# Buffers, root operations, weight-part order and store queues in a two-layer encoder kernel

## The chip, the cores and the metric

The kernel runs on one core of a Trainium2 chip. The metric is the device time of one launch in microseconds (us). The profile calls the engines PE (TensorE: matrix products; PEld is its weight load), DVE (VectorE), ACT (ScalarE), POOL (GpSimd) and SP (SyncE, which here only issues DMAs). SPq and ACTq are the parts of SP and ScalarE that issue DMAs.

## The reference

One inference step of a two-layer encoder on 1024 prompt frames and 64 frames of a running stream, 1088 columns in all, 1024 features each, in float32. Layer 0 is a state-space mixer, layer 1 is banded attention; each is followed by a gated feed-forward block (FFN). Norms stand ahead of and behind every block. Cut to what the change touches:

```python
def rmsnorm(x, w):
    y = x * lax.rsqrt(jnp.mean(x * x, axis=-1, keepdims=True) + EPS)
    return y * w

def swiglu(u, w_in, w_out):                 # w_in: 1024 x 5632, w_out: 2816 x 1024
    g, up = jnp.split(u @ w_in, 2, axis=-1)
    return (jax.nn.silu(g) * up) @ w_out

def shared_kv(x, kv_norm_w, w_kv):
    kv = (rmsnorm(x, kv_norm_w) @ w_kv).reshape(b, L, 2, ATT_HEADS, ATT_HEAD_DIM)
    return kv[:, :, 0], kv[:, :, 1]

# one layer, mix = ssd_mixer (layer 0) or the band attention of q, k, v (layer 1):
x = x + rmsnorm(mix(rmsnorm(x, nw[0])), nw[1])
x = x + rmsnorm(swiglu(rmsnorm(x, nw[2]), w_in, w_out), nw[3])
```

The K, Q and V of layer 1 are made from the stream after layer 0, 16 heads of 64.

## The kernel before, in words

Every tensor lies with features on the partitions and the 1088 columns along the free side. A float32 product runs as three passes on TensorE: each operand is split into a high part (a cast to fp32r, on ScalarE) and a low part (what is left, a subtraction on VectorE), and hi·hi, hi·lo and lo·hi are summed in PSUM. In `W.part` (L386, L387) this is done for weights: `hl` or `half` is the split, `raw` the loaded weight, `tt` a sum of weight blocks.

The order of TensorE's instructions is written out by the program: a stream of products, and small tasks (`st.spawn`, `st.run`) that are put between them at planned times. The other engines' order is set by a scheduler which builds each queue from the same program by data readiness and priority (`tc.high_priority(n)`; HIP is 3000). An engine then works through its queue strictly in order and waits at the head of it.

**FFN.** The columns go in two parts, b=0 and b=1 (`HO`, 544 columns in two halves each). The hidden features are 22 tiles. Products are built in 2x2 blocks with seven block products instead of eight (P1 to P7), for which sums of weight blocks and of activation blocks are formed ahead. `T_PLAIN` are the six tiles which run without that scheme for b=0 at the start (`plain_pairs`); `T_BOTH` are the 16 tiles that run in the scheme for both parts, "first pair" being the first of them; `T_TAIL` are the six plain tiles' b=1 parts, which run at the end of the up-projection, the tail. `W` makes the weight blocks' sums and splits, at priority `W.pri`; their keys are names of blocks ("ta", "tb" are sums). `op_build` makes the activation blocks: `total` forms sums and `split` the two parts (cast L1247, subtraction L1248), with priority `OPP`. In `run_pair` the gates and their products are evicted (L1427 to L1444: `p`, `c`, `u`, `x`). `hidden` takes the finished hidden tile, forms four sums of its blocks on GpSimd (L1481), and stores seven blocks to DRAM (L1475, `hscr`), on ScalarE's DMA queue for `T_PLAIN` tiles and on SP's for the others. For the down-projection they are loaded again (L1512) and split (L1518, L1519), partly while the tail still runs. SP's queue also loads the weights (L283), each of which waits for a free `raw` buffer.

**Attention entry.** In `back`, four column quarters q=0..3 of layer 0's result are finished. `rb_steps` calls `rstd` for the inverse root of the mean square: a reduction and L576 on VectorE, then seven small VectorE operations (L580 to L588: a bit-trick start and a cubic polynomial) on a tile of 2 or 3 columns, `nv`, into `nr`; `bcast` spreads `nr` over the partitions through TensorE (`nbp`, L594) and a ScalarE copy. Then the projections follow in three column slices of up to 384. Their evictions `evk`, `evq` and `evv` multiply the PSUM tile by the root into `kf`, `qf` and `vt` (L1898, L1924, L1952), which share one ring of tiles, tag "kqv". `kf` and `qf` are split further into K, Qh and Ql (copies among partitions on SP, L1930), `vt` is transposed, and `kf` and `vt` are also stored as outputs (L492). `cr` and `Cv` are loads of the cached keys and values, `Ck` the cast keys (L1869); `bias` tiles are loaded and partly set by GpSimd memsets (L1885, L1886). The attention task computes scores (L1990), exponentials (L2004) and transposes (`ptp`, L2020).

Of the kernel before, what the change touches and what calls it, by code (L numbers as in the profile page):

```python
# [16 lines left out]
P = 128  # L17
D = 1024
# [22 lines left out]
NS = mybir.DependencyInfo(mybir.DependencyClass.NoSync, mybir.DependencyReason.DATA)  # L41
# [9 lines left out]
EP_W, ER_W, EQ_W = (6.0, 5.0, 8.0, 6.0), (6.0, 4.0, 6.0, 5.0), (16.0, 11.5, 18.0, 16.0)  # L51
# [201 lines left out]
class Weights:  # L253
# [4 lines left out]
    def __init__(self, nc, raw, hl, half, tt):  # L258
        self.nc, self.raw, self.hl, self.half, self.tt = nc, raw, hl, half, tt

        self.tc, self.pri, self.nsc = None, 0, 0
        self.lq, self.sq, self.ready, self.eng = [], [], [], None

        self.raws, self.lent = [raw], None

        self.hx, self.used = Ring(None, "hx", 0, hl.shape, hl.dtype), []

# [99 lines left out]
    def part(self, it, key, ring, v, eng=None, acc=None):  # L367
        if it.get("held"):
            ring = self.held
        elif ring is not self.half:  # L370
            ring = self.hl if ring or self.hl.free() else self.hx
            self.used.append(ring)
        t, n = ring.get(), v.shape[1]
        h, lo = t[:, 0, :n], t[:, 1, :n]
        if it.get("acc"):
            acc = it["src"][0]
        if acc is not None and acc is not False:

            with self.tc.high_priority(self.pri):
                self.nc.scalar.copy(h, v)  # L380
                self.nc.scalar.activation(lo, h, AF.Copy, scale=-1.0)
            self.nc.gpsimd.dma_start(lo, acc, accum_op=ALU.add)
            it[key] = h, lo
            return
        with self.tc.high_priority(self.pri):
            self.nc.scalar.copy(h, v)  # L386
            (eng or self.eng or self.nc.vector).tensor_tensor(lo, v, h, op=ALU.subtract)  # L387
        it[key] = h, lo

# [33 lines left out]
def hybrid_kernel(  # L423
# [60 lines left out]
    def paced(x):  # L484
        if at_pe[0] is not None:
            tc.add_manual_dep(x.ins, at_pe[0].ins.name, NS, reason="pace")
        return x
# [68 lines left out]
            A.activation(q[:, :n], src, AF.Square)  # L556
            (eng or G).tensor_tensor(ssum[:, :n], ssum[:, :n], q[:, :n], op=ALU.add)  # L557

    def rstd(ssum, inv, r, nb, more=None):

        sp = ax("nst")
        if more is None:
            for i in range(nb):
                PE.transpose(sp[:, i * P:(i + 1) * P], ssum[:, i * P:(i + 1) * P], ident)
        else:
            for j, t in enumerate((ssum, more)):
                for i in range(nb):
                    c = 4 * j + i
                    PE.matmul(sp[:, c:c + 1], t[:, i * P:(i + 1) * P], ones[:, 0:1], start=True, stop=True)
        with tc.high_priority(HIP):  # L570
            v = nss.tile([P, 12], F32, tag="nv", bufs=2, name="nv")
            a, h, y = v[:, 0:nb], v[:, 4:4 + nb], v[:, 8:8 + nb]
            if more is None:
                sums = sp[:, :nb * P].rearrange("p (a b) -> p a b", b=P)
                V.tensor_reduce(a, sums, axis=mybir.AxisListType.X, op=ALU.add)
                V.tensor_scalar(a, a, inv, EPS, op0=ALU.mult, op1=ALU.add)  # L576
            else:
                V.tensor_scalar(a, sp[:, :nb], inv, EPS, op0=ALU.mult, op1=ALU.add)
                V.scalar_tensor_tensor(a, sp[:, 4:4 + nb], inv, a, op0=ALU.mult, op1=ALU.add)
            V.tensor_scalar(y.bitcast(I32), a.bitcast(I32), -0.5, float(0x5F3759DF), op0=ALU.mult, op1=ALU.add)  # L580
# [7 lines left out]
            V.scalar_tensor_tensor(r, a, RP[3], y, op0=ALU.add, op1=ALU.mult)  # L588
# [8 lines left out]
        A.activation(rb[:, :n], bp[:, a:a + n], AF.Copy, scale=RL)  # L597
        return rb[:, :n]

    def rb_steps(ssum, n, out, wait=None, rb=None, more=None):  # L600

        nb = (n + P - 1) // P
        nr = nss.tile([P, 4], F32, tag="nr", bufs=2, name="nr")
        rstd(ssum, 1.0 / D, nr[:, :nb], nb, more)
# [610 lines left out]
    def op_build(ops, done, when=lambda: True):  # L1215
# [22 lines left out]
        def split(nm_, keep=False):  # L1238
            if nm_ == "a21":
                yield 0, 0, lambda: R.free(2)  # L1240
                got = [(R.get(), R) for _ in range(2)]
            else:
                yield 0, 0, lambda: some(2)
                got = [take(*rings) for _ in range(2)]
            h, l_ = (rr(v4(t, n)) for t, _ in got)
            with tc.high_priority(OPP[ops.layer][ops.b]):
                A.copy(h, L[nm_])  # L1247
                V.tensor_tensor(l_, L[nm_], h, op=ALU.subtract)  # L1248
# [206 lines left out]
    def back(layer, start, cpost, xsrc, xmid, cpre, cpost2, xout, rb_out, done2):  # L1455
# [3 lines left out]
        with ExitStack() as es:  # L1459
# [6 lines left out]
            def hidden(t_, b, x, z, late=None):  # L1466
# [5 lines left out]
                    st.spawn(store(i, t), HST)  # L1472

                def store(i, t):
                    paced((A if t_ in T_PLAIN else nc.sync).dma_start(hc[:, i, k, HO[b]:HO[b] + n], t))  # L1475
                    stored[i, b] = stored.get((i, b), 0) + 1
                    return
                    yield
# [64 lines left out]
            def end(q, y, ss, more=None):  # L1543
# [76 lines left out]
                    if q in qs and all(x in parts for x in qs):  # L1620
                        done2.append(s)
                yield (0, EQ_W[q]) if q < 3 else (0, 0, lambda: "k2" in done2)
                yield from rb_steps(tot, n, [], ER_W[q], rb_out[:, o:o + n])
                roots.append(q)
                for s, qs in enumerate(((0, 1), (1, 2), (2, 3))):
                    if q in qs and all(x in roots for x in qs):
# [2 lines left out]
            with e2:  # L1629
# [25 lines left out]
                for t_, bs, ends in [(t_, (0, 1), (0,) if t_ == T_BOTH[-1] else ()) for t_ in T_BOTH] + [(t_, (1,), (1,) if t_ == T_TAIL[-1] else ()) for t_ in T_TAIL]:  # L1655
# [4 lines left out]
                        t_, W.get(), bs, ends, ops, lambda *a: hidden(*a, late=late[1] if one else None), px, tmp,  # L1660
                        t_ == T_BOTH[0], late[0] if one else None,
                    )
                    W.pri = 0
                    if t_ == T_BOTH[-1]:
                        phase[0] = 1
                        W.lent.cap = 2
# [181 lines left out]
    with ExitStack() as es:  # L1848
# [41 lines left out]
        def evk(j):  # L1890
            d = kqv[j]

            def f(s, p_):
                n = SL[s][1]
                st.wait_for(lambda: ("rb", s) in done)
                kf = sb2.tile([P, 384], F32, tag="kqv", bufs=2, name="kf")
                with tc.high_priority(HIP):
                    V.tensor_tensor(kf[:, :n], p_[:, :n], rba[s][:, :n], op=ALU.mult)  # L1898
                if not d["Kt"]:
# [13 lines left out]
        def evq(j):  # L1913
            def f(s, p_):
# [4 lines left out]
                if s == 2:  # L1919
                    for q_ in Q[0] + Q[1]:  # L1920
                        G.memset(q_[:, n:].bitcast(F32), 0.0)
                qf = sb2.tile([P, 384], F32, tag="kqv", bufs=2, name="qf")
                with tc.high_priority(HIP):
                    V.scalar_tensor_tensor(qf[:, :n], p_[:, :n], 0.125, rba[s][:, :n], op0=ALU.mult, op1=ALU.mult)  # L1924
                for e in range(2):
# [20 lines left out]
        def evv(j):  # L1946
            def f(s, p_):
                o, n = SL[s]
                st.wait_for(lambda: ("rb", s) in done)
                vt = sb2.tile([P, 384], F32, tag="kqv", bufs=2, name="vt")  # L1950
                with tc.high_priority(HIP):
                    V.tensor_tensor(vt[:, :n], p_[:, :n], rba[s][:, :n], op=ALU.mult)  # L1952
                if s == 1:
# [391 lines left out]
```

## Time and profile before

| | |
|---|---|
| median of 3 runs | 2901.99 us (2899.79 to 2910.09) |
| the profiled execution | 2901.95 us, span 2900.2 us, mean granted clock 0.996 |
| TensorE busy | 98% of the span, 22096 matmuls |
| VectorE busy | 77%, 4767 instructions |
| ScalarE busy | 46%, 2411 |
| GpSimd busy | 26%, 927 |
| DMA | 443.22 MB, 153 GB/s in the mean |

A busy time is summed over an engine's instructions. A wait row names the waiting instruction, the one that released it, and the total, number and longest of such waits. In the timeline a row is start, duration, engine, line, operation, output and inputs; in brackets stands the idle time ahead of it and its releaser. The granted clock is the share of full speed that TensorE got. On the profile's clock layer 0's first pair lies at 905 to 935 us and its tail at 1255 to 1330; the attention entry at 1540 to 1625; layer 1's first pair at 2235 to 2265 and its tail at 2585 to 2660.

### The profile page before, as it was taken

How to read it: one execution, taken by the hardware profiler on the slowest of the kernel's cores; microseconds unless marked ns; L12 is line 12 of the kernel's file. 1: busy time of each engine (PE TensorE's matmuls, PEld its weight loads, DVE VectorE, ACT ScalarE, POOL GpSimd, SP SyncE). 2: the span in 40 equal slices, each digit the busy share in tenths (PEclk: the TensorE clock that was granted, in tenths of full speed). 3: DMA queues.
4: the chain of work that ended last, by engine and by line, in shares of the span. 5: the costliest groups of instructions: out<-in, count | busy, mean ns of one | idle time of the engine just before them, and what ended most of it. 6: DMA issues, size and time to landing. Idle time of an engine off the chain costs nothing. (4 is left out here: it accounts for less than half of the span.)

```text
span 2900.2 us, 57727 instructions
## 1 busy us (share of the span) xinstructions
PE 2843.5 (98%) x22096; PEld 2799.6 (97%) x22096; DVE 2242.8 (77%) x4767; ACT 1347.7 (46%) x2411; POOL 763.6 (26%) x927
## 2 busy tenths in 40 slices
PE   8999999999999999999999999999999999999999
PEld 8999999999999999999999899999999999999998
DVE  7987888786768877787678777777778877787456
ACT  6654646454444222235444455555664322234342
POOL 1343333330123434342022000000032434343012
PEclk9999999999999999999999999999999999999999
DMA  4433333235565455557875432223367454565555
GB/s 134 129 103 99 106 102 108 89 121 159 171 175 165 156 172 168 175 192 262 288 226 179 131 91 77 66 66 89 98 213 217 148 177 148 183 201 191 193 184 159
DMA packets 284789, 443.22 MB, mean 153 GB/s; under 512 B 25696, under 2 KB 231488, under 8 KB 283104
## 3 DMA queue, kind: packets, MB, share of 16 engines
q1 hardware_dynamic: 269184, 417.27, 44.8%
q0 software_dynamic: 3232, 10.56, 2.0%
q10 hardware_dynamic: 12096, 11.70, 1.2%
q8 instruction: 173, 2.83, 0.4%
q14 instruction: 104, 0.85, 0.1%
HBM read 321.34 MB, written 113.63 MB: 150 GB/s over the span
## 5 line engine op out<-in xcount | busy, mean ns | idle before, releaser
L531 PE MATMUL mm<-r,hl 128*128 128x384 f32 (+2 forms) x1672 | 556.4, 333 | 6.1 <-DVE kf L1898 5.0
L533 PE MATMUL mm<-r,hl 128*128 128x384 f32 (+2 forms) x1672 | 539.2, 322 | 1.2 <-DVE hl L387 0.7
L532 PE MATMUL mm<-r,hl 128*128 128x384 f32 (+2 forms) x1672 | 539.0, 322 | 0.0
L1416 PE MATMUL px<-r,hl 128*128 128x288 f32 (+1 forms) x1184 | 348.1, 294 | 0.0
L531 PEld LDWEIGHTS mm<-r,hl 128*128 128x128 f32 x1672 | 316.4, 189 | 8.7 <-DVE kf L1898 5.7
L1417 PE MATMUL px<-r,hl 128*128 128x288 f32 x1056 | 312.4, 296 | 5.4 <-DVE hl L387 5.4
L533 PEld LDWEIGHTS mm<-r,hl 128*128 128x128 f32 x1672 | 315.6, 189 | 1.9 <-DVE hl L387 1.0
L532 PEld LDWEIGHTS mm<-r,hl 128*128 128x128 f32 x1672 | 316.6, 189 | 0.3
L1415 PE MATMUL px<-r,hl 128*128 128x288 f32 x1056 | 311.7, 295 | 2.1 <-DVE u L1430 1.6
L387 DVE TENSOR_TENSOR hl<-raw,hl 128x1024 fp32r<-128x1024 f32 (+2 forms) x186 | 209.5, 1128 | 118.4 <-ACT hl L386 118.1
L557 POOL TENSOR_TENSOR ssum<-ssum,sq 128x256 f32<-128x256 f32 (+1 forms) x111 | 124.5, 1122 | 562.6 <-ACT sq L556 547.8
L386 ACT CAST hl<-raw 128x1024 fp32r<-128x1024 f32 (+2 forms) x186 | 177.4, 954 | 125.2 <-PE po L1758 66.9
L1416 PEld LDWEIGHTS px<-r,hl 128*128 128x128 f32 x1184 | 223.1, 188 | 0.0
L1417 PE MATMUL px<-rx,hl 128*128 128x256 f32 x768 | 214.8, 280 | 6.5 <-DVE hl L387 6.5
L1415 PE MATMUL px<-rx,hl 128*128 128x256 f32 x768 | 214.4, 279 | 1.3 <-DVE x L1389 1.3
L1417 PEld LDWEIGHTS px<-r,hl 128*128 128x128 f32 x1056 | 199.4, 189 | 6.4 <-DVE hl L387 6.4
L1415 PEld LDWEIGHTS px<-r,hl 128*128 128x128 f32 x1056 | 199.5, 189 | 3.3 <-DVE u L1430 2.1
L1756 PE MATMUL po<-r,hl 128*128 128x288 f32 (+1 forms) x682 | 196.8, 288 | 0.0
L1757 PE MATMUL po<-r,hl 128*128 128x288 f32 (+1 forms) x682 | 196.4, 288 | 0.0
L1758 PE MATMUL po<-r,hl 128*128 128x288 f32 (+1 forms) x682 | 196.4, 288 | 0.0
L1416 PE MATMUL px<-rx,hl 128*128 128x256 f32 x640 | 178.9, 280 | 0.0
L2004 ACT ACTIVATE sc<-sc,mx 128x640 f32<-128x640 f32 (+3 forms) x144 | 101.8, 707 | 107.9 <-DVE mx L1999 102.2
(444 smaller groups left out, 8436.6 us busy)
## 6 DMA issues: line engine op xcount, KB each, us to landing
raw<-in_w_f_dram SPq DMA_DIRECT2D x104, 512.0 KB, 4.0
wsum<-in_w_f_dram SPq DMA_DIRECT2D x128, 176.0 KB, 3.7
wscr<-wsum SPq DMA_DIRECT2D x128, 176.0 KB, 3.3
raw<-in_w_in_dram SPq DMA_DIRECT2D x40, 512.0 KB, 3.7
MT<-ascr SPq DMA_DIRECT2D x48, 384.0 KB, 4.2
raw<-in_w_so_dram SPq DMA_DIRECT2D x32, 512.0 KB, 3.9
r<-hscr SPq DMA_DIRECT2D x22, 576.0 KB, 6.2
hl<-kscr SPq DMA_DIRECT2D x11, 1024.0 KB, 5.2
```

Source lines behind the costliest of these rows:

```text
L386: self.nc.scalar.copy(h, v)
L387: (eng or self.eng or self.nc.vector).tensor_tensor(lo, v, h, op=ALU.subtract)
L531: PE.matmul(ps[:, :n], h_, xh, start=(first and i == 0), stop=False)
L532: PE.matmul(ps[:, :n], h_, xl, start=False, stop=False)
L533: at_pe[0] = PE.matmul(ps[:, :n], l_, xh, start=False, stop=(last and i == nk - 1))
L557: (eng or G).tensor_tensor(ssum[:, :n], ssum[:, :n], q[:, :n], op=ALU.add)
L1415: PE.matmul(ps, wh, ah[:, k, :], start=(k == 0), stop=False)
L1416: PE.matmul(ps, wh, al[:, k, :], start=False, stop=False)
L1417: at_pe[0] = PE.matmul(ps, wl, ah[:, k, :], start=False, stop=(k == 3))
L1756: PE.matmul(ps[:, :n], wh, xh, start=(k == 0), stop=False)
L1757: PE.matmul(ps[:, :n], wh, xl, start=False, stop=False)
L1758: at_pe[0] = PE.matmul(ps[:, :n], wl, xh, start=False, stop=(k == KH - 1))
```

## The change

It has five parts. The "kqv" ring has four buffers instead of two. The roots at the attention entry (`rb_out`) are computed on GpSimd: the seven VectorE operations become eleven, since each scalar_tensor_tensor becomes two operations. A split of b=1's activation blocks in `op_build` is ordered behind the last "tb" cast (an order in ScalarE's queue, no wait between engines). `W.pri` is 1000 and no longer 0 from the second pair on. The stores of `hidden` for b=1 go by SP's queue also for `T_PLAIN` tiles.

```diff
         with self.tc.high_priority(self.pri):
-            self.nc.scalar.copy(h, v)
+            last = self.nc.scalar.copy(h, v)
+            if key == "tb":
+                self.last = last
             (eng or self.eng or self.nc.vector).tensor_tensor(lo, v, h, op=ALU.subtract)
...
+            if eng is not None:
+                eng.tensor_scalar(y.bitcast(I32), a.bitcast(I32), -0.5, float(0x5F3759DF), op0=ALU.mult, op1=ALU.add)
+                eng.tensor_tensor(h, y, y, op=ALU.mult)
+                eng.tensor_tensor(h, h, a, op=ALU.mult)
+                for i, p in enumerate(RP):
+                    eng.tensor_scalar(a, a if i else h, p, None, op0=ALU.add)
+                    eng.tensor_tensor(r if i == 3 else a, a, y if i == 3 else h, op=ALU.mult)
+                return
             V.tensor_scalar(y.bitcast(I32), a.bitcast(I32), -0.5, float(0x5F3759DF), op0=ALU.mult, op1=ALU.add)
...
             with tc.high_priority(OPP[ops.layer][ops.b]):
-                A.copy(h, L[nm_])
+                first = A.copy(h, L[nm_])
+                if ops.b and W.last is not None:
+                    tc.add_manual_dep(first.ins, W.last.ins.name, NS, reason="order")
                 V.tensor_tensor(l_, L[nm_], h, op=ALU.subtract)
...
-                    paced((A if t_ in T_PLAIN else nc.sync).dma_start(hc[:, i, k, HO[b]:HO[b] + n], t))
+                    paced((A if t_ in T_PLAIN and not b else nc.sync).dma_start(hc[:, i, k, HO[b]:HO[b] + n], t))
...
-                yield from rb_steps(tot, n, [], ER_W[q], rb_out[:, o:o + n])
+                yield from rb_steps(tot, n, [], ER_W[q], rb_out[:, o:o + n], eng=G)
...
-                    W.pri = 0
+                    W.pri = 1000
...
-                kf = sb2.tile([P, 384], F32, tag="kqv", bufs=2, name="kf")
+                kf = sb2.tile([P, 384], F32, tag="kqv", bufs=4, name="kf")
...
-                qf = sb2.tile([P, 384], F32, tag="kqv", bufs=2, name="qf")
+                qf = sb2.tile([P, 384], F32, tag="kqv", bufs=4, name="qf")
...
-                vt = sb2.tile([P, 384], F32, tag="kqv", bufs=2, name="vt")
+                vt = sb2.tile([P, 384], F32, tag="kqv", bufs=4, name="vt")
```

The order of TensorE's instructions is the same in both kernels. VectorE has 28 instructions fewer, ScalarE's queue 42 DMAs fewer, SP's 42 more, GpSimd 44 operations more. The changed kernel's lines are two to twelve higher (L386 stays, L1247 becomes L1257, L1475 becomes L1487, L1518 L1530, L492 L494, L1884 L1896).

ScalarE's queue at layer 0's first pair, before. The casts of L1247 are b=1's; `tt_11088` is the last "tb" sum.

```order
L386 CAST hl_11168<-tt_11087 128x1024
L380 CAST half_11243<-raw_11102 128x512
L1247 CAST r_11256<-r_9050 128x1152
L381 ACTIVATE half_11243<-half_11243 128x512
L1475 DMA hscr0_114<-x_10942 128x256
L1475 DMA hscr0_114<-sg_11080 128x256
L1247 CAST r_11283<-r_9051 128x1152
L1247 CAST r_11314<-r_11065 128x1152
L386 CAST hl_11236<-tt_11088 128x1024
```

The same place after:

```order
L386 CAST hl_11168<-tt_11087 128x1024
L380 CAST half_11243<-raw_11102 128x512
L1487 DMA hscr0_114<-x_10942 128x256
L381 ACTIVATE half_11243<-half_11243 128x512
L1487 DMA hscr0_114<-sg_11080 128x256
L386 CAST hl_11236<-tt_11088 128x1024
L1257 CAST r_11256<-r_9050 128x1152
L1439 COPY p1_11266<-px_11249 128x256
L1257 CAST r_11283<-r_9051 128x1152
```

The cast of `tt_11088` now stands ahead of three of the L1247 casts, which were ahead of it.

ScalarE's queue in the tail of layer 0, before. `p`, `px` are evictions of the pair, `hl`, `half` weight parts, `hscr` the stores.

```order
L1475 DMA hscr_114<-c_15756 128x288
L1475 DMA hscr_114<-rx 128x288
L1433 ACTIVATE p_15816<-p_15816 128x288
L386 CAST hl<-rx 128x1024
L386 CAST hl<-tt 128x1024 x2
L1443 ACTIVATE px<-px 128x288
L386 CAST half<-raw 128x512
L1427 COPY p_15947<-px 128x288
L1475 DMA hscr_114<-c_15887 128x288
L1475 DMA hscr_114<-rx 128x288
```

The same place after:

```order
L1439 COPY p_15816<-px 128x288
L386 CAST hl<-rx 128x1024
L1445 ACTIVATE p_15816<-p_15816 128x288
L386 CAST hl<-tt 128x1024 x2
L1455 ACTIVATE px<-px 128x288
L386 CAST half<-raw 128x512
L1439 COPY p_15947<-px 128x288
L386 CAST hl<-rx 128x1024
```

The stores are gone from this queue, and a weight cast stands ahead of the activation of `p`.

SP's queue at the attention entry, before. `kscr` are parts of the K and V weights.

```order
L492 DMA x2d<-y 128x4x288
L1930 DMA Ql_19511<-Ql_19511 64x384
L1930 DMA Ql_19513<-Ql_19513 64x384
L1884 DMA bias<-in_rbrow_dram 128x640 x2
L492 DMA out_vT_dram<-vt 128x256
L1867 DMA cr<-in_ckT_dram 64x512 x2
L1884 DMA bias<-in_rbrow_dram 128x640
L492 DMA out_kT_dram<-kf 128x256
L307 DMA hl<-kscr_134 128x2048
```

The same place after:

```order
L494 DMA x2d<-y 128x4x288
L1942 DMA Ql_19523<-Ql_19523 64x384
L1942 DMA Ql_19525<-Ql_19525 64x384
L1896 DMA bias<-in_rbrow_dram 128x640
L494 DMA out_vT_dram<-vt 128x256
L1942 DMA Ql_19550<-Ql_19550 64x384
L1942 DMA Ql_19552<-Ql_19552 64x384
L494 DMA out_kT_dram<-kf 128x256
L1896 DMA bias<-in_rbrow_dram 128x640
L1875 DMA Cv<-in_cv_dram 128x4x128
L1879 DMA cr<-in_ckT_dram 64x512 x2
L307 DMA hl<-kscr_134 128x2048
```

The loads of `Cv` and `cr` now stand behind the second two `Ql` copies, the first store of `kf` and a second `bias` load.

More of the change, by code (lines that the diff above doesn't have):

```diff
@@ L262, in __init__ @@
         self.lq, self.sq, self.ready, self.eng = [], [], [], None
-        self.raws, self.lent = [raw], None
+        self.raws, self.lent, self.last = [raw], None, None
         self.hx, self.used = Ring(None, "hx", 0, hl.shape, hl.dtype), []
@@ L557, in add_sq, with rstd @@
             (eng or G).tensor_tensor(ssum[:, :n], ssum[:, :n], q[:, :n], op=ALU.add)
-    def rstd(ssum, inv, r, nb, more=None):
+    def rstd(ssum, inv, r, nb, more=None, eng=None):
         sp = ax("nst")
@@ L598, in bcast, with rb_steps @@
         return rb[:, :n]
-    def rb_steps(ssum, n, out, wait=None, rb=None, more=None):
+    def rb_steps(ssum, n, out, wait=None, rb=None, more=None, eng=None):
         nb = (n + P - 1) // P
         nr = nss.tile([P, 4], F32, tag="nr", bufs=2, name="nr")
-        rstd(ssum, 1.0 / D, nr[:, :nb], nb, more)
+        rstd(ssum, 1.0 / D, nr[:, :nb], nb, more, eng)
         yield 0.3, wait or RB_WAIT
```

## The prediction

> **What bounds the kernel now.** I read the busy times first, then TensorE's waits, then the granted clock over short windows, and last, at each wait, the queues of the engine it waits for.
>
> ```profile
> PE 2843.5 (98%) x22096; PEld 2799.6 (97%) x22096; DVE 2242.8 (77%) x4767; ACT 1347.7 (46%) x2411; POOL 763.6 (26%) x927
> PE px L1417 <- DVE hl L387: 11.9, 7, 2.4
> PE mm L531 <- DVE kf L1898: 5.0, 2, 4.3
> PE nbp L594 <- DVE nr L588: 4.8, 5, 1.6
> ...
> 927.50:930.90 3.40, 3.40 (x18) 3.40 (x17) 1.57 (x5) 0.79 (x2) 1.48 (x2) 0.50 0.53 137
> 1603.30:1610.10 6.80, 6.05 (x23) 6.05 (x24) 5.89 (x16) 5.81 (x12) 0.00 (x0) 0.50 0.30 95
> 2603.40:2606.80 3.40, 3.40 (x17) 3.40 (x16) 3.40 (x4) 1.21 (x2) 0.80 (x1) 0.50 0.63 238
> 2253.00:2259.00 6.00, 5.31 (x44) 5.31 (x45) 5.95 (x7) 2.52 (x4) 4.66 (x3) 1.00 0.18 50
> ```
>
> TensorE is busy for 2843.5 of 2900.2 us. No matmul is added, dropped or reordered, so the change can win only from the idle rest, about 57 us, and from time at half clock. The wait rows (us in total, times, longest) say where the edits can reach: weight parts `hl` made by VectorE (11.9 us), the K split `kf` (5.0), the root's `nr` (4.8). The windows (length; busy of PE, PEld, DVE, ACT, POOL; granted clock; DMA share; GB/s) add a second price. Behind three of the waits the clock was 0.50, and busy time there is half work: 3.40/2 = 1.7 us lost, 6.05/2 = 3.0, and 1.7. The fourth window, behind a wait as long as the first one's, stayed at 1.00: a dip is not certain.
>
> [...]
>
> **First pair of each FFN** (edit: the splits of the second half are put behind the "tb" cast).
>
> ```profile
> 922.00 1.04 ACT L386 CAST hl<-tt 128x1024 fp32r<-128x1024 f32 x1
> 922.98 1.35 DVE L1248 TENSOR_TENSOR r<-r 128x1152 fp32r<-128x1152 f32 x1
> 924.25 1.75 DVE L387 TENSOR_TENSOR hl<-tt,hl 128x1024 fp32r<-128x1024 f32 x1
> 926.05 0.38 PE L1417 MATMUL px<-rx,hl 128*128 128x256 f32 x1 [2.36 <-DVE hl L387]
> 2253.69 0.38 PE L1417 MATMUL px<-rx,hl 128*128 128x256 f32 x1 [2.37 <-DVE hl L387]
> ```
>
> In layer 0 the last sum's cast stands behind three casts of L1247 on ScalarE, its subtraction behind L1248 splits of 1.35 us on VectorE, and the matmul waits 2.36 us. The new order puts cast and subtraction ahead of all three. Two splits fewer on either engine are 2.7 us, more than the gap, so gap and dip go: 2.36 + 1.7 = −4.1 us (0 to −4.1). In layer 1 only one L1248 moves behind: −1.35, taken as −1.3 (0 to −2.4). The splits are wanted by the second half of the first pair, and hide behind its first half; if they came late, they would return up to the 1.35 us of one.
>
> **Tails of the FFNs** (edits: weight parts get priority 1000 after the first pair; the second half's hidden stores leave ScalarE's queue for SP's).
>
> ```profile
> 1255.00:1330.00 75.00, 71.36 (x538) 70.54 (x537) 68.24 (x97) 35.24 (x50) 41.85 (x31) 1.00 0.59 190
> 1271.29 1.68 DVE L1519 TENSOR_TENSOR rx<-rx 128x768 fp32r<-128x768 f32 x1
> 1274.76 0.40 PE L1417 MATMUL px<-r,hl 128*128 128x288 f32 x1 [1.54 <-DVE hl L387]
> 1296.65 1.26 POOL L1481 TENSOR_TENSOR rx<-c,rx 128x288 f32<-128x288 f32 x1
> 1297.94 0.33 ACTq L1475 DMA_DIRECT2D hscr<-rx  x1
> 1298.66 1.03 ACT L386 CAST hl<-rx 128x1024 fp32r<-128x1024 f32 x1
> 1299.73 1.23 DVE L387 TENSOR_TENSOR hl<-rx,hl 128x1024 fp32r<-128x1024 f32 x1 [1.19 <-ACT hl L386]
> 1311.04 0.40 PE L1415 MATMUL px<-r,hl 128*128 128x288 f32 x1 [1.37 <-DVE u L1430]
> 2602.89 0.40 PE L1417 MATMUL px<-r,hl 128*128 128x288 f32 x1 [2.43 <-DVE hl L387]
> ```
>
> Two causes show. A split of the hidden rows (L1519, 1.68 us) stands ahead of the subtraction the matmul waits for. And ScalarE's queue holds a store that needs GpSimd's product (ends 1297.91, store 1297.94), with the next weight cast behind it, for which VectorE idled 1.19 us. Both go: the subtraction moves ahead of the split, and 42 stores leave ScalarE. In layer 0 the gaps are 1.54 + 1.37 = 2.9 us; in layer 1 the one shown is 2.43, with its 1.7 of dip. But VectorE is busy for 68.24 of 75 us in this stretch: the split passed over is late next, and the hidden matmuls want it. Its idle 6.8 us exceed what PE would save, though not by much once the stretch is shorter, so I take two thirds of the gaps: layer 0 −1.9 (0 to −2.9), layer 1 −1.6 − 1.7 = −3.3 (0 to −4.1).
>
> On SP the 42 stores wait for the same GpSimd products, with weight loads (L283) behind them.
>
> ```profile
> 1261.84 0.99 SPq L1475 DMA_DIRECT2D hscr<-u  x2
> SPq L283 <- ACT half L386: 14.5, 3, 7.0
> ```
>
> One store takes 0.5 us to issue, so 21 of them 10.4 us a layer. In the tail SP stands waiting for free slots far longer (14.5 us for ScalarE's half casts alone), so I cost this at nothing; gone, that cover leaves 0 to +5 us a layer.
>
> **Attention entry** (edit: four buffers where `kf`, `qf` and `vt` shared two).
>
> ```profile
> 1600.29 0.56 DVE L1924 SCALAR_TENSOR_TENSOR qf<-kq,rbf 128x384 f32<-128x384 f32 x1 [3.46 <-DMA out_vT_dram<-vt]
> 1600.63 0.62 ACT L1869 CAST Ck<-cr 64x512 fp32r<-64x512 f32 x1 [7.64 <-DMA cr<-in_ckT_dram]
> 1604.05 0.64 PE L531 MATMUL mm<-r,hl 128*128 128x320 f32 x1 [4.30 <-DVE kf L1898]
> ```
>
> `qf` waits 3.46 us until the store of an old `vt` has left its buffer; `kf` takes its turn behind it, and only then is the PSUM bank free in which the next product is to be built: 4.30 us of PE, and then the dip. With four buffers the `vt` isn't in the way. So the gap and the dip go: 4.30 + 3.0 = −7.3. What is late next is the cached K. In the new order SP issues its load `cr` behind two more `Ql` copies, the store of K, a bias and `Cv`: five more, at 0.5 us each by the store's row above 2.5 us. The cast moves from 1600.63 to past 1603, the first exponentials stand behind it on ScalarE, and TensorE, 7.3 us ahead, wants them sooner: lateness of up to 2.5 us, less a margin that I can't read, +1.0 (0 to +2.5, or +5 with a new dip). Net −6.3 (−7.3 to −2).
>
> **Small root operations on GpSimd** (seven VectorE operations become eleven, four times).
>
> ```profile
> 1578.35 0.17 DVE L580 TENSOR_SCALAR nv<-nv 128x2 int32<-128x2 int32 x1
> 1582.01 0.16 DVE L588 SCALAR_TENSOR_TENSOR nr<-nv 128x2 f32<-128x2 f32 x1
> 1582.31 0.40 PE L594 MATMUL nbp<-ident,nr 128*128 128x128 f32 x2 [1.16 <-DVE nr L588]
> 1612.75 0.17 DVE L580 TENSOR_SCALAR nv<-nv 128x3 int32<-128x3 int32 x1
> 1614.34 0.16 DVE L588 SCALAR_TENSOR_TENSOR nr<-nv 128x3 f32<-128x3 f32 x1
> 1615.41 0.49 PE L594 MATMUL nbp<-ident,nr 128*128 128x128 f32 x3
> ...
> 74.99 0.18 POOL L841 COPY halo<-craw 128x3 f32<-128x3 f32 x1 [6.70 <-DVE craw L813]
> 75.23 0.18 POOL L836 COPY craw<-halo 128x3 f32<-128x3 f32 x1
> L836 POOL COPY craw<-halo 128x3 f32<-128x3 f32 x48 | 16.4, 342 | 9.5 <-DVE BT L853 5.4 <-DVE nv L576 1.3
> 1558.83 3.56 POOL L557 TENSOR_TENSOR ssum<-ssum,sq 128x288 f32<-128x288 f32 x1 [5.23 <-ACT sq L556]
> ```
>
> GpSimd runs no such chain now. The nearest rows: a dependent pair of small copies at a pace of 0.24 us, and the same copy's mean of 0.342 us, 0.41 with the 0.06 between two. Eleven are 2.7 to 4.5 us. At the second quarter the chain took 1582.17 − 1578.35 = 3.8 us amid other VectorE work, and PE waited 1.16. By the group's mean, since VectorE is dense there: +0.7 (−1.1 to +1.7, at 0.5 each). At the fourth it took 1.75 us in quiet, with 0.9 to spare; by the pair's pace, and with two memsets in between, 2.7 + 0.3 − 1.75 − 0.9 = +0.4 (0 to +2.9). The first and third have room. Sum +1.1.
>
> [...]
>
> **Sum.** −4.1 −1.3 −1.9 −3.3 −6.3 +1.1 = −15.8. The profiled execution took 2901.95 us (span 2900.2 and 1.75 around it), within 0.1 of the median 2901.99, so the forecast is 2886.1, in round numbers 2886. No change can be told within 0.5%, 14.5 us: faster begins at 2887.5, and the likely case straddles that. Its own range is 2880 (every term at its better end: −4.1 −2.4 −2.9 −4.1 −7.3 −1.1 = −21.9) to 2894 (half the sum).
>
> **Rivals.**
> First, the waits are handed on. VectorE is 91% busy in the tails; the hidden splits passed over come late for hidden matmuls, and late `cr` holds the entry. The tails then give 0, the entry −3, the first pairs −4, the chains +1.1: 2896. For it speaks 68.24 of 75; against it that PE's order gives the splits more lead than the weights. Chance 0.20.
>
> Second, on the other side: GpSimd's chain is held by VectorE. With p the time from one of its operations to the next, the second quarter's chain loses 11p − 3.8 and the fourth's 11p + 0.3 − 1.75 − 0.9; with the third's put like the fourth's, that is 33p − 8.5. Each stall then also risks a dip of 1.7 to 3.0, say 7 in all. To undo the other −16.9 and end slower by 14.5 takes 33p − 8.5 + 7 = 31.4, so p over 1.0 us. At 1.1 the time is 2920. L836's longest of 1.7 us and the 3.56 above speak for it; the mean of 0.34 against. Chance 0.05.
>
> Third, SP's stores block the weight loads: 5 us a layer off a gain of 15.8 leaves 2896. For it: loads stand right behind the stores. Against: SP's long waits. Chance 0.06.
>
> Fourth, a priority or an ordering that isn't a wait changes nothing that matters, since the engines' queues keep much of their order: only the entry counts, −5.2, 2897. The rows' new order speaks against it. Chance 0.05.
>
> Fifth, a better end than the likely one: the idle 57 us hold waits that I left alone, and VectorE and ScalarE, with 28 and 42 instructions fewer, close some of these too: 22 us, 2880 or below. Chance 0.12.
>
> **Chances.** The likely case has 0.52; its centre is 1.4 us under the bound, so 0.35 of it counts as faster and 0.17 as within 0.5%. Faster is 0.35 + 0.12 = 0.47. Slower is the second rival's 0.05, and 0.01 for a first rival with new dips. The rest, 0.47, lies within. The range leaves out the second rival and a tenth of the others: 2875 to 2899.
>
> **What would show it.** Right: no wait over 1 us for `hl` in the two first pairs and tails; clock 1.00 where it was 0.50; `qf` without a wait for a store; no 288-wide store in ScalarE's queue; chains of L583 to L588 on GpSimd in under 4.5 us, and a wait of `nbp` of at most 2. Wrong: new PE waits for `rx` or `r` splits in the tails, for `ptp`'s input at the entry, for `raw` loads behind SP's stores; GpSimd operations of 1 us; new half-clock windows.

## The result, and the profile after

The changed kernel takes 2895.43 us (median of 13 runs, 2891.59 to 2899.03) where the kernel before, beside it, took 2902.88 (2899.79 to 2910.09): ratio 0.9971, 95% interval 0.9963 to 0.998. A second set of executions gave 0.9965 (0.9953 to 0.9978). The gain is 8.4 us by the ratio. Forecast were 15.8, a time of 2886, and a range from 2875 to 2899. The time lies in the range, but half of the gain is missing.

The page of the changed kernel, its first lines (span; busy times):

```profile
span 2893.7 us, 57789 instructions
...
PE 2843.4 (98%) x22096; PEld 2799.2 (97%) x22096; DVE 2227.5 (77%) x4739; ACT 1347.6 (47%) x2411; POOL 772.8 (27%) x971
```

TensorE's waits in the changed kernel (us in total, times, longest):

```profile
PE nbp L604 <- POOL nr L588: 4.3, 2, 3.4
...
PE px L1429 <- DVE hl L389: 2.9, 2, 2.4
...
PE mm L533 <- DMA hl<-kscr: 2.4, 1, 2.4
...
PE mm L533 <- DVE kf L1910: 0.7, 1, 0.7
```

The waits that the change aimed at are gone or small: `hl` from 11.9 us to 2.9, `kf` from 5.0 to 0.7. Two rows are new: TensorE waits 4.3 us for GpSimd's roots, and 2.4 us for a load of K and V weights. Windows over the changed kernel show half clock behind both, and behind the wait that is left in layer 1's first pair:

```profile
1579.00:1582.50 3.50, 3.50 (x14) 3.41 (x14) 1.97 (x5) 3.13 (x7) 0.00 (x0) 0.52 0.57 201
...
1606.00:1609.50 3.50, 3.50 (x15) 3.50 (x16) 1.99 (x7) 1.16 (x4) 2.60 (x11) 0.56 0.61 255
...
2243.50:2247.00 3.50, 3.30 (x19) 3.30 (x20) 3.50 (x5) 3.50 (x5) 2.12 (x2) 0.68 0.24 56
```

TensorE runs the same matmuls in the same order in both kernels, so each one's start can be set against its own in the other profile. The lead at a few of them gives the account by place (us; minus is gain):

| place | one matmul's start, before and after | lead there | change in this stretch | forecast |
|---|---|---|---|---|
| ahead of layer 0's first pair | 912.58, 912.09 | −0.5 | −0.5 | 0 |
| behind that pair | 933.24, 929.61 | −3.6 | −3.1 | −4.1 |
| end of its tail | 1315.62, 1308.42 | −7.2 | −3.6 | −1.9 |
| start of the down-projection | 1345.45, 1339.70 | −5.8 | +1.4 | 0 |
| third quarter's root | 1590.17, 1589.25 | −0.9 | +4.8 | +0.7 |
| behind the wait for `kf` | 1610.14, 1601.91 | −8.2 | −7.3 | −7.3 |
| behind the K/V load | 1613.72, 1609.49 | −4.2 | +4.0 | +1.4 |
| attention, to its end | 2108.20, 2104.97 | −3.2 | +1.0 | 0 |
| behind layer 1's first pair | 2259.39, 2257.09 | −2.3 | +0.9 | −1.3 |
| end of its tail | 2644.14, 2637.41 | −6.7 | −4.4 | −3.3 |
| end of the span | 2900.2, 2893.7 | −6.5 | +0.2 | 0 |

(The forecast's +1.0 for the cached K and +0.4 for the fourth quarter stand together in the row of the K/V load.) Two profiles of one kernel differ by up to 1.9 us in a single stretch, and by more ahead of the change: the matmul at 912.58 starts between 909.96 and 917.57 in the 14 profiles of this document, although every engine's queue holds the same instructions in the same order up to there. So the places tell more than the times. Two rows are furthest off, and both lie at the attention entry: the roots of the second and third quarter, and the K/V load.

### The profile page after: what moved, and what is told of

It is laid out like the page before. It is cut to its first block, busy times and chain, and to the rows that moved or that the text cites. A ratio compares the mean times of both kernels' runs of the same rounds, so it can differ in the third digit from the quotient of the medians.

```text
span 2893.7 us, 57789 instructions
## 1 busy us (share of the span) xinstructions
PE 2843.4 (98%) x22096; PEld 2799.2 (97%) x22096; DVE 2227.5 (77%) x4739; ACT 1347.6 (47%) x2411; POOL 772.8 (27%) x971
## 5 line engine op out<-in xcount | busy, mean ns | idle before, releaser
L386 ACT CAST hl<-raw 128x1024 fp32r<-128x1024 f32 (+2 forms) x186 | 177.5, 955 | 116.2 <-PE po L1770 72.3
```

Of the source, the lines that this page charges most:

```text
L386: last = self.nc.scalar.copy(h, v)
```

## The experiments

**The roots back on VectorE.** The change without its second part.

```diff
-                yield from rb_steps(tot, n, [], ER_W[q], rb_out[:, o:o + n], eng=G)
+                yield from rb_steps(tot, n, [], ER_W[q], rb_out[:, o:o + n])
```

> The change without its root part: the four roots at the attention entry stay on VectorE, the other four parts are in. Theory: the gain that is missing was lost by the GpSimd chains of the second and third quarter, which a run of VectorE operations with two SBUF inputs holds up (nbp waits 3.37 and 0.93 us and half clock behind the first; together 4.8 us later than TensorE's place in the profile of before). Then those waits are gone and the kernel takes 2891 us, 4 to 5 less than the changed kernel; TensorE reaches the third slice about 5 us sooner. Since the loads of Cv and the cached K then also stand earlier in SP's queue, the 2.35 us wait for a K/V weight load may shrink, to 2888 at best. Rival (what the prediction's small price of +1.1 says): the chains on GpSimd cost about 1 us, what is lost is lost by half clock that falls at random: 2894 to 2896.

Measured: 2890.89 us (2886.05 to 2894.67), ratio 0.9943 (0.993 to 0.9957). That is 0.0022 to 0.0028 below the changed kernel's two ratios, 6 to 8 us, give or take 5 by the intervals. The wait for the K/V load did not shrink, as was thought possible, but grew to 3.37 us. Why a chain is dear is seen in the changed kernel itself. Its timeline on GpSimd in the second quarter's chain (start, duration):

```profile
1573.14 3.13 POOL L585 TENSOR_TENSOR nv<-nv 128x2 f32<-128x2 f32 x1
1576.36 0.22 POOL L587 TENSOR_SCALAR nv<-nv 128x2 f32<-128x2 f32 x1
...
1578.41 0.20 POOL L588 TENSOR_TENSOR nr<-nv 128x2 f32<-128x2 f32 x1
...
1586.83 1.27 POOL L588 TENSOR_TENSOR nv<-nv 128x3 f32<-128x3 f32 x1
```

and on VectorE beside it:

```profile
1573.35 0.46 DVE L1553 TENSOR_TENSOR r<-y,r 128x288 fp32r<-128x288 f32 x1
1573.72 1.35 DVE L1597 TENSOR_TENSOR y<-y,r 128x1152 f32<-128x1152 f32 x1
1574.99 1.19 DVE L1553 TENSOR_TENSOR r<-y,r 128x288 fp32r<-128x288 f32 x3
1576.10 0.21 DVE L1553 TENSOR_TENSOR r<-strip,r 128x32 fp32r<-128x32 f32 x1
...
1586.69 1.36 DVE L1626 TENSOR_TENSOR y<-y 128x1152 f32<-128x1152 f32 x1
```

L585 works on two columns and stays on the engine for 3.13 us, until 1576.27. VectorE has a closed row of operations with two SBUF inputs there which ends at 1576.31; the next GpSimd operation takes 0.22. In the third quarter an operation of 1.27 us ends at 1588.10, VectorE's L1626 at 1588.05. The second chain took 6.35 to 6.43 us and the third 6.45 to 6.47 in six profiles of kernels that have it.

The times go with the kind of VectorE's operation beside them. In the changed kernel, one GpSimd operation beside a VectorE operation that reads PSUM (`po`), which took 0.22 us, and one beside a subtraction of two SBUF tiles, which took 0.61:

```profile
1541.36 0.22 POOL L587 TENSOR_SCALAR nv<-nv 128x2 f32<-128x2 f32 x1
1541.21 0.46 DVE L1718 TENSOR_TENSOR y<-po,y 128x288 f32<-128x288 f32 x1 [1.36 <-PE po L1770]
...
1606.11 0.61 POOL L583 TENSOR_SCALAR nv<-nv 128x3 int32<-128x3 int32 x1 [5.54 <-DVE nv L578]
1605.98 0.69 DVE L1882 TENSOR_TENSOR Ck<-cr,Ck 64x512 fp32r<-64x512 f32 x1
```

Counted over the 286 root operations on GpSimd in seven profiles: the 84 that overlap a VectorE operation with two SBUF inputs took 0.28 to 3.21 us, and each ended 0.05 to 0.09 us behind the end of such an operation. The 80 beside other VectorE work took 0.19 to 0.31 us, the 122 beside none 0.19 to 0.23.

**Four buffers alone.** The kernel before with one edit.

```diff
-                kf = sb2.tile([P, 384], F32, tag="kqv", bufs=2, name="kf")
+                kf = sb2.tile([P, 384], F32, tag="kqv", bufs=4, name="kf")
...   (qf and vt alike)
```

> The kernel before with four buffers for kf, qf and vt as the only edit. The prediction's term: -7.3 for the wait and the half clock, +1.0 for the late cached K: 2896.6 against 2902.9, ratio 0.9978. Theory now: the wait for qf goes, but a load of K/V weights (hl<-kscr) is late next, because its buffer comes free only with TensorE's progress and its landing takes 5 us and more: net -3 to -4, about 2899.5. No wait of GpSimd's root chains here, since the roots stay on VectorE: the second and third quarter must look as before.

Measured: 2904.59 us beside 2906.39, ratio 0.9993 (0.9984 to 1.0002): no gain that can be told, where 3 to 4 us were expected. The timeline, on TensorE and on SP:

```profile
1611.95 0.41 PE L531 MATMUL mm<-r,hl 128*128 128x320 f32 x1 [3.71 <-DMA hl<-kscr]
...
1603.72 0.38 SPq L307 DMA_DIRECT2D hl<-kscr  x1
```

The 4.30 us wait for `kf` is replaced by one of 3.71 for `hl`, with half clock behind it in turn. The load's product starts 8.2 us after its issue. Against the kernel before, TensorE gains 7.3 us at `kf` and gives 6.1 back at the load. In the kernel before, the same load and the product that wants it:

```profile
1599.78 0.33 SPq L307 DMA_DIRECT2D hl<-kscr  x1
...
1611.67 0.30 PE L531 MATMUL mm<-r,hl 128*128 128x320 f32 x1
```

There 11.9 us lie between the two, and the load is never waited for.

**The cached K and V loaded first.** The run with the roots on VectorE, and

```diff
+            with tc.high_priority(HIP):
                 nc.sync.dma_start(Cv, ...)      # and both cr loads alike
```

> As the run with the roots on VectorE, and the loads of the cached K and V (cr, Cv) get a high priority, so that they stand in SP's queue ahead of the stores, the second Ql copies and the bias loads. If the wait for the K/V weight load at the entry comes from those loads sharing the DMA engines with it, its landing goes back from 7.1 to about 5 us and the wait from 2.35 to under 1, with no half clock behind it: 2 to 3 us less than that run. If its late issue alone decides (the buffer comes free late), nothing changes against that run.

Measured: 2891.29 us, ratio 0.9947 (0.9935 to 0.996), the same as without it. The edit also moved the three bias loads:

```profile
1593.25 1.54 SPq L1898 DMA_DIRECT2D bias<-in_rbrow_dram  x3
1594.89 0.38 SPq L307 DMA_DIRECT2D hl<-kscr  x1
...
1602.68 0.63 PE L533 MATMUL mm<-r,hl 128*128 128x320 f32 x1 [2.90 <-DMA hl<-kscr]
```

Now three bias tiles of 320 KB stand right ahead of the load, and the wait is 2.90. This told less than hoped: one set of neighbours had taken the place of another.

**The third bias behind the load.** On top of that, the first two bias tiles get the high priority too, and the next pair's first bias load is ordered behind the K/V load.

```diff
-        self.nc.sync.dma_start(t.bitcast(F32), src)
+        self.klast = self.nc.sync.dma_start(t.bitcast(F32), src)
...
-                nc.sync.dma_start(bt, ...)
+                with tc.high_priority(0 if j else HIP):
+                    bl = nc.sync.dma_start(bt, ...)
+                if j == 1 and e == 0:
+                    tc.add_manual_dep(bl.ins, W.klast.ins.name, NS, reason="order")
```

> Roots on VectorE, and the K/V weight load at the entry gets the DMA engines for itself: the cached K and V and the first two bias tiles are loaded before it, the third bias tile behind it. Theory: in all kernels with four buffers the load is issued when its buffer comes free, 4.6 us of matmuls before it is wanted, and lands after 7 to 8 us because some 0.6 MB of small loads and copies share the engines; with them away it lands in about 5 and the wait of 2.9 to 3.7 us falls to about 1 or none, and no half clock follows: 3 to 4 us less than with the roots on VectorE alone, about 2887 where that is 2891. Rival: 1 MB needs its 7 us anyway, and the wait stays above 2.5.

Measured: 2884.5 us (2881.21 to 2886.28), ratio 0.9927 (0.9913 to 0.9941); the changed kernel beside it took 2895.24. The timeline on SP and TensorE, and the load's size and median time to landing in 1588 to 1606 us:

```profile
1586.63 0.49 SPq L1881 DMA_DIRECT2D cr<-in_ckT_dram  x1
1593.19 0.33 SPq L307 DMA_DIRECT2D hl<-kscr  x1
...
1598.90 0.41 PE L533 MATMUL mm<-r,hl 128*128 128x320 f32 x1 [0.96 <-DMA hl<-kscr]
...
hl<-kscr SPq DMA_DIRECT2D x3, 1024.0 KB, 5.7
```

In the changed kernel these loads land more slowly (stretch 1590 to 1616):

```profile
hl<-kscr SPq DMA_DIRECT2D x3, 1024.0 KB, 7.1
```

The wait falls to 0.96 us, and TensorE's lead over the run with the roots on VectorE grows by 4.3 us there, wait and half clock together. The two times alone don't show it: the ratios, 0.9927 and 0.9943, have overlapping intervals. In all twelve profiles with four buffers this load is issued 4.5 to 5.0 us ahead of its need. It landed after 6.3 to 8.2 us in the nine where bias tiles, `Cv` or `cr` are issued close to it, and after 5.4 to 5.7 in the three where they are not. So most of the wait was the company that the load had; the rest is its late issue.

**The changed kernel timed beside this one.** No edit.

> The changed kernel, timed beside the next three on one chip. Theory: the root chains on GpSimd cost 4 to 5 us, so it is at a ratio of 0.996 to 0.9975 to the kernel before, against 0.9943 for the run with the roots on VectorE. Rival (the chains cost about 1 us): within 0.0006 of that run.

Measured: 0.9965 (0.9953 to 0.9978), as the theory has it; its GpSimd chains make TensorE wait 3.45 and 0.31 us.

**Weight priority back at 0.**

```diff
-                    W.pri = 1000
+                    W.pri = 0
```

> The changed kernel with the priority of weight parts back at 0 from the second pair on; the store queues and the order behind the tb cast stay. Theory: the waits for hl in the tails (1.54 us in layer 0, 2.43 in layer 1 and half clock there) come from a split of hidden rows ahead of the weight's subtraction, which the priority alone sets right: they return, 3 to 6 us more than the changed kernel. Rival: the stores' move from ScalarE is what freed them, and the time stays within 1 us.

Measured: 2896.23 us, ratio 0.9969 (0.9957 to 0.9981), not told apart from the changed kernel's 0.9965. The profile tells more than the time. Both waits are back, at their places:

```profile
1268.91 0.40 PE L1429 MATMUL px<-r,hl 128*128 128x288 f32 x1 [1.45 <-DVE hl L389]
...
2598.88 0.41 PE L1429 MATMUL px<-r,hl 128*128 128x288 f32 x1 [2.30 <-DVE hl L389]
...
2596.00:2604.00 8.00, 5.70 (x43) 5.47 (x42) 8.00 (x10) 3.39 (x5) 3.58 (x4) 1.00 0.84 302
```

But no half clock followed (1.00 in the window). Against the changed kernel TensorE lost 0.9 us in layer 0's tail and 1.3 in layer 1's, less than the 3.75 us of the two waits, and less than the 3 to 6 expected.

**Stores back in ScalarE's queue.**

```diff
-  paced((A if t_ in T_PLAIN and not b else nc.sync).dma_start(...))
+  paced((A if t_ in T_PLAIN else nc.sync).dma_start(...))
```

> The changed kernel with the second part's hidden stores of the tail back in ScalarE's queue. Theory: the two long waits for hl stay away (they hang on the priority), the waits of 1.37 us for u and 0.72 for hl at the end of layer 0's tail return, since a weight cast again stands behind a store that waits for GpSimd: 1 to 3 us more than the changed kernel. The rival on SP's queue in the prediction (stores block loads) would make it faster, by 2 to 5 us.

Measured: 2894.57 us, ratio 0.9967 (0.9958 to 0.9976): the same, and not the 1 to 3 us more that were expected. No wait of TensorE over 0.2 us shows in either tail. With priority 0 and stores on SP, the waits for `u` (1.37) and for `hl` (0.72) in layer 0's tail were gone as well. The kernel before, profiled again, has 0.2 us in place of the 1.37 and a wait of 1.39 in layer 1's tail, so a single profile doesn't show what took that one away. Against the kernel before, TensorE gains 5.8 us in the two tails with the stores moved and priority 0, 6.9 with priority 1000 and the stores back, and 8.0 with both. (Of the 5.8, some 1.7 is half clock that did not come, though its wait did.) Either edit brings most of the gain; the second one adds little.

**No order behind the tb cast.**

```diff
-                if ops.b and W.last is not None:
+                if False and W.last is not None:
```

> The changed kernel without the order of the second part's splits behind the tb cast. Theory: the 2.36 us wait for hl in layer 0's first pair returns (gone in all runs with the order), TensorE is 2.3 to 4 us later from there on, by half clock or not; in layer 1 the wait of 2.4 returns in place of one of 0.6: 1.5 to 2 us. Together 4 to 6 us more than the changed kernel. Rival: the priority of weight parts alone would do it too, and the time stays within 1 us.

Measured: 2899.75 us, ratio 0.9983 (0.9974 to 0.9992), 3.5 to 5 us above the changed kernel by the ratios. TensorE's waits at layer 0's first pair:

```profile
PE px L1429 <- DVE hl L389: 2.9, 2, 2.4
PE px L1427 <- DVE x L1401: 1.6, 1, 1.6
```

The 2.36 us wait is back, in layer 1 one of 2.37; TensorE falls back by 4.4 us at the first and by about 1.0 at the second.

**Roots on GpSimd only in the first and fourth quarter.** On the version with the third bias late.

```diff
+  ..., rb_out[:, o:o + n], eng=G if q in (0, 3) else None)
```

> As the run with the third bias late, but the roots of the first and the fourth quarter on GpSimd, those of the second and third on VectorE. Theory: a chain costs what VectorE's neighbours with two SBUF inputs make of it. The second and third quarter, with dense neighbours, took 6.4 us each in four profiles; the fourth 4.05 in a quieter place, which its slack nearly covers. So the time stays within 1.5 us of the run with the third bias late (2884.5 there) and no wait for nr of over 1.2 us comes up. Rival: the chain itself is too long on GpSimd whatever runs beside it: a wait of 2 us and more at the fourth quarter.

Measured: 2886.61 us, ratio 0.9937 (0.9924 to 0.9951), not told apart from 0.9927. The fourth chain's ends and TensorE's wait:

```profile
1602.16 0.20 POOL L583 TENSOR_SCALAR nv<-nv 128x3 int32<-128x3 int32 x1 [11.84 <-DVE nv L578]
...
1605.14 0.20 POOL L588 TENSOR_TENSOR nr<-nv 128x3 f32<-128x3 f32 x1
...
1605.39 0.54 PE L604 MATMUL nbp<-ident,nr 128*128 128x128 f32 x3 [1.16 <-POOL nr L588]
```

Eleven operations take 3.2 us here (3.1 in the first quarter), 0.29 apart, against 6.4 in the dense quarters. With TensorE ahead, the fourth quarter's slack is used up and 1.16 us of wait come up. Half clock follows from 1607.42 to 1610.84, and TensorE's lead falls by 2.7 us over this place, while it holds in the run with the third bias late. So in this profile even a chain in a quiet place cost more than it freed.

**The best so far with the stores on ScalarE.** The edit of the stores again, on the version with the third bias late.

> The best so far (roots on VectorE, third bias late) with the tail's stores back in ScalarE's queue, where they cost nothing in the run before: within 2 us of 2884.5, ratio about 0.9925; the small waits at the start of layer 0's down-projection (0.78 and 0.36 us) are gone. Rival (the stores' move is worth 1 to 3 us, as the prediction had it): 2886 to 2888.

Measured: 2887.33 us (2882.46 to 2890.05), ratio 0.9936 (0.9923 to 0.995). The time is one that the rival gives, but the interval overlaps that of 0.9927, so neither is told apart. In the profile the tails gain 1.3 us less than with the stores on SP, and the start of the down-projection 0.5 more.

**Both kernels profiled a second time.** No edit in either.

> The changed kernel a second time, one look. Theory: the waits are set by the order and return to 0.3 us; where the clock halves is not fully set by them, so one or two stretches of half clock (at the root chain of the second quarter, behind the K/V load, at layer 1's first pair) may be missing or shifted, each worth about 1.7 us. Rival: the same stretches return at the same places.

> The kernel before a second time, one look. The same waits at the same places to 0.3 us: 2.36 at layer 0's first pair, 4.3 at the entry, 1.5 and 2.4 in the tails. If half clock behind a wait of 2.4 us is chance, at least one of the three stretches of half clock is missing or another has come up; the rival, that it is set by the length of the wait alone, has them at the same three places.

Times: 2892.5 and 2904.37 us. In the second profile of the changed kernel the waits for the second quarter's root and for the load were 3.46 and 2.76 us (3.37 and 2.35 in the first), the second without half clock behind it; at layer 1's first pair the first `hl` wait was 1.17 instead of 2.36, again without half clock, and TensorE gained 1.2 us on the first profile there. In the kernel before, the windows behind layer 0's tail wait and layer 1's tail wait, first profile:

```profile
1274.80:1278.20 3.40, 3.40 (x26) 3.40 (x27) 3.40 (x5) 1.79 (x4) 1.28 (x1) 1.00 0.92 344
...
2603.00:2606.40 3.40, 3.40 (x16) 3.40 (x17) 3.40 (x5) 1.61 (x3) 1.20 (x1) 0.56 0.76 286
```

and second profile:

```profile
1276.30:1279.70 3.40, 3.36 (x14) 3.36 (x15) 3.40 (x5) 1.77 (x3) 1.29 (x1) 0.54 1.04 402
...
2605.60:2609.00 3.40, 3.40 (x25) 3.40 (x26) 3.40 (x5) 1.78 (x4) 1.29 (x1) 1.00 0.77 292
```

The waits return (1.54 and then 2.07 us; 2.43 and then 2.31), the half clock has changed places.

The traces show a grid in its places. From the first stretch of half clock on, every change of the granted clock in a trace lies on a grid of 3.4133 us, to 6 ns over a whole execution and in all 14 traces. Where the grid starts differs from one execution to the next. Windows of this grid around three waits, the kernel before, first profile:

```profile
924.07:927.48 3.41, 1.43 (x12) 1.43 (x13) 3.41 (x6) 0.00 (x0) 3.33 (x3) 1.00 0.08 28
927.48:930.90 3.42, 3.42 (x18) 3.42 (x18) 1.59 (x5) 0.79 (x2) 1.50 (x2) 0.50 0.53 137
...
2251.86:2255.27 3.41, 1.58 (x13) 1.58 (x14) 3.41 (x6) 0.12 (x1) 3.33 (x3) 1.00 0.03 11
2255.27:2258.68 3.41, 3.41 (x30) 3.41 (x30) 3.35 (x2) 2.39 (x3) 2.47 (x2) 1.00 0.23 77
2600.02:2603.43 3.41, 0.98 (x8) 0.74 (x7) 3.41 (x5) 1.23 (x2) 2.25 (x3) 1.00 1.06 402
2603.43:2606.84 3.41, 3.41 (x16) 3.41 (x16) 3.41 (x4) 1.18 (x2) 0.77 (x1) 0.50 0.62 233
```

The wait of 2.36 us has 1.98 us in one window (TensorE busy for 1.43 of 3.41), and the next window runs at half clock. The wait of 2.37 us begins at 2251.32, so 0.54 of it fall into the window before and 1.83 into this one (busy 1.58), and the clock stays at 1.00. The wait of 2.43 us lies in one window as a whole. Counted over the 14 traces from 100 us on, windows at half clock themselves left out: all 35 windows with 1.93 us or more of idle TensorE were followed by half clock, 3 of the 10 with 1.73 to 1.93 us, 4 of the 28 with 1.36 to 1.73 us (all at 704 to 711 us), and none of the others. So in these traces half clock went with the idle time within one window, and not with the length of the wait: it came behind 2.36 us and stayed away behind 2.37.

TensorE's time over five stretches, less that in the first profile of the kernel before, over all 14 profiles (us):

| stretch | with the edit | without it |
|---|---|---|
| first pair of layer 0 (order behind the "tb" cast) | −3.0 to −3.8 in ten | 0 to +2.0 in four |
| both tails (priority and stores) | −6.8 to −8.2 in eight; one of the two edits alone −5.8 to −6.9 in three | 0 to +1.9 in three |
| roots of the second and third quarter on GpSimd | +3.6 to +5.2 in six | −0.6 to +0.6 in eight |
| `kf` (four buffers) | −7.2 to −7.4 in twelve | 0 and −1.4 |
| K/V load (four buffers) | +1.9 to +5.6 in nine; with the third bias late +1.0 to +1.2 in three | 0 in both |

## Why the prediction was right or wrong

It was right on the direction, on the places of the old waits and on what each is released by, and wrong on the size. Two steps failed, both at the attention entry: the price of the chains on GpSimd, and a load of K and V weights that the removed wait had covered and that has no term in the sum. That the time lies in the range is partly luck: the tails gained 2.8 us more than forecast. And 2895.4 is close to the 2896 of the first and third rivals and the 2897 of the fourth, but none of their mechanisms came.

**Small root operations on GpSimd: +1.1 forecast, +4.8 in the profile, 6 to 8 in the timed ratios.** The step that failed is "By the group's mean, since VectorE is dense there: +0.7". The pace of one operation, 0.41 us, was the mean of copies that stand alone or beside all sorts of work; in the second quarter's dense place one operation of the eleven took 3.13 us beside a closed row of VectorE's operations with two SBUF inputs, and ended 0.09 us behind one of them. In quiet the pace was 0.29, near the pair's 0.24. "The first and third have room" was wrong for the third: its 6.46 us overran the room it had, by 0.93 us of wait. The second rival, that VectorE holds the chain, fits the 84 operations above, at a little over half its strength: the dense quarters' chains took 0.58 us an operation, where its loss of 14.5 us needed 1.0. (By its own formula a p of 0.56 us would have undone the other gains; but it gives the third and fourth chains each a loss of 11p − 2.35, 4 us here, and TensorE waited 0.93 us for the third and not at all for the fourth.) Of the rows that were to speak for it, the longest of L836 is 1.23 us; the 1.7 is one of L841. The prediction's sum for a chain, 2.7 to 4.5 us, was below the measured 6.4.

**Attention entry: −7.3 came in full, the wait behind it was another.** "So the gap and the dip go" held (−7.2 to −7.4 at that place in twelve profiles). It is a gain on the first profile of the kernel before, where 6.83 us of half clock followed the wait; in the second, 3.41 followed, and the place cost 1.4 us less. "What is late next is the cached K" did not hold: no wait for `Ck` shows. Late next was a 1 MB weight load, and the step that I left out is that the old wait had given it time. Before, it was issued at 1599.78 and wanted at 1611.67; with four buffers alone it was issued at 1603.72 and wanted at 1611.95 − 3.71 = 1608.24, 4.5 us later, less than the 5.4 that it took at best. So where +1.4 was forecast, +4.0 came. Four buffers alone gave 0.9993, and the order of the small loads around it gave most of the rest back.

**First pairs.** In layer 0 −4.1 was forecast; −3.1 came in the first profile, −3.0 to −3.8 in ten, and 4.4 went when the order was taken out. In layer 1 the wait went (from 2.37 to 0.6 at most), but an earlier one, which the forecast left alone, ate the gain: 1.78 and 2.64 us in the two profiles of the kernel before, 2.36 in the changed kernel with half clock behind it, and from none to 3.09 us over the runs.

**Tails: −5.2 forecast, −8.0 less 1.4 handed on in the profile.** "Two thirds" was too careful: VectorE had room. But the two causes were not to be added. "ScalarE's queue holds a store" was true and mattered little once the priority was right, and the priority mattered little once the stores were gone: one edit alone left 5.8 to 6.9 of the 8.0 us. The third rival's 5 us a layer did not show, since the kernel with the stores back was no faster. The rival of handed-on waits shows as +1.4 at the down-projection's start, not as the whole 5.2 us of the tails.

**The chance of half clock.** The sum took 1.7 us of half clock as lost and regained with two waits of about 2.4 us. In the 14 traces half clock came whenever 1.93 us or more of a window on the grid were idle (35 of 35). A wait of 2.4 us puts that much into one window at a little over half of the places it can have on a grid of 3.41 us (an estimate from the measured 1.93 and 3.41 us: 2 × (2.4 − 1.93) + 3.41 − 2.4 = 1.95 us out of 3.41), so about half of 1.7 us is what the half clock behind such a wait costs on average, by this estimate.

What stays open: why GpSimd gets in between two of VectorE's operations at some places, and at another (L585, 3.13 us) not until most of a row of six has passed; and what goes with half clock when between 1.36 and 1.93 us of a window are idle. The timed cost of the chains (6 to 8 us, give or take 5) is less sharp than the profiles' 3.6 to 5.2 for the second and third quarter.

## What to carry to other kernels

Before taking away a long wait, ask of every transfer issued during it when it would be wanted without it; the one with the least time left is the next wait, and the small loads that stand ahead of it can often go elsewhere, which here was worth about 4 us in the profile, half of what the change gained. A chain of tiny dependent operations should not be costed by the mean of such operations (a pace of 0.41 us by it here, where 0.58 came in the dense quarters): look at which operations VectorE runs in that very stretch. Two edits against the same waits should not be added up before each has run alone. And where the time can't tell parts of a change apart, the start of one and the same matmul in two profiles can.

## What the runs showed of the hardware

An operation of GpSimd on 128x2 or 128x3 elements took 0.19 to 0.23 us alone (122 of the 286 counted); the 84 beside a VectorE operation with two SBUF inputs took 0.28 to 3.21 and ended 0.05 to 0.09 us behind the end of such an operation; beside a closed row of six, 3.13 to 3.21 us, in six profiles. A load of 1 MB landed in 5.7 us with few neighbours and in 7.1 with about 1 MB of small ones (the store of K, a bias tile, `Cv`, two `cr`). The granted clock changed on a grid of 3.4133 us whose start differs between executions. Half clock followed waits of TensorE of 2.07, 2.36 and 2.43 us, which had 1.98 us and more in one window, and did not follow waits of 2.30, 2.31 and 2.37, which were split between two windows with 1.83 us at most in either.
